# Encoder layer in split fp32 on one core: neighbouring weight pairs multiplied in alternation, and the work beside them spread out

## The chip, the core and the metric

The kernel runs on one core of a Trainium2 chip. TensorE (PE) multiplies, PEld is its loading of the stationary operand; VectorE (DVE), ScalarE (ACT) and GpSimd (POOL) compute, SyncE (SP) issues loads, and POOL also issues the stores. The metric is the device time of one execution in microseconds. The kernel before takes 2571.83 us (median of 3 runs, 2565.88 to 2572.41).

## The reference, cut to what matters

One layer for 512 prompt tokens and 2048 sample tokens, all fp32, 1024 channels:

```
h = rmsnorm(x, norm_pre);  z = h @ w_in                 # 1024 -> 6656
pool_u, pool_g, q, k, v, attn_g, merge = split(z)
pb = (multiscale_pool(pool_u) per group @ w_pool_group) * pool_scale * silu(pool_g)
ab = windowed_attention(rope(q), rope(k), v, sink) * silu(attn_g)
m = sigmoid(merge_p) * (pb @ w_pool_proj) + sigmoid(merge_a) * (ab @ w_attn_proj)
y = x + rmsnorm(m @ w_out, norm_post)
```

The change touches the first half alone: the norm, the projection `z`, and what is done with each column of `z` before it is stored.

## The kernel before, in words

Every fp32 operand is split in two parts, hi and lo (`hi_lo`: ACT rounds it to fp32r, DVE subtracts), and a product is three matmuls (`mm3`, lines 143 to 145).

**Phase 1** is the input projection. The 2560 tokens stand in three blocks (768, 896, 896), the 6656 columns in 26 pairs of 2 x 128 columns. A block times a pair is a 2 x 2 product of halves with seven multiplications in place of eight, M1 to M7, in the order `ORDER = M1, M6, M2, M5, M7, M3, M4`. One such product is 12 matmuls (four slices of K by three) with 384 or 448 moving columns. Its operands are sums of quarters: `X[...]` of the tokens, which lie in `arena` for a block, and `A11, A12, A22, S1` to `S4` of the weights, split product by product into one of seven `w` tiles (`Pair.op`).

Products accumulate in three PSUM banks of a pair: A (`ps_g`, two buffers) holds M1 and then M1+M2, B (`ps_s`, three buffers) M6, then M5, then M3 on top, C M7 and then M4 (`ps_s`, for the second of two joined pairs `ps_o`, of which there is one). After each product something reads the bank, and the next product into the same bank must wait for that reader: M2 waits for `s` (ACT, line 441), M5 for `U2` (DVE, line 444), M3 for `U4` (DVE, line 452), M4 for the sum after M7 (DVE, line 424). In the order above one other product stands between a product and the one that waits for its reader. After M4 `post.finish()` does what the columns need: `Rope` (k and q: six DVE operations on 896 columns, two splits, sixteen stores), `Silu`, `Gate`, `Pool`, `Values`. A pair's results lie in two `z` tiles from its M2 on until they are stored; `finish` takes up to two more, and there are six.

TensorE runs in the order in which the program is written (`manual_schedule`); the other engines' order is set by the framework's scheduler, and each engine runs its queue strictly in that order. `run` issues the weight splits up to seven `w` tiles ahead.

**Beside the products** stands other work, hung into the program with `hook` and `beside` at a pair and product of a block: squares of the next block's tokens for the norm (`stats_load`, `stats_sum`), forming the next block's token sums (`later_load`, `later_form`, pairs 9 to 17), the pooling of the first block's columns (`late_load`, `late_pool`, from block 1, pair 13), and the splitting of the second phase's weights (`split_load`, `split_form`, block 2, pairs 6 to 23). All of them load into the four `h` tiles. A piece is loaded at one product and used three products later.

**The start.** `first_stats` squares the first block's eight token slices on ACT, and TensorE sums each over the partitions (48 matmuls against `ones`). Then `rstd`, `prep_r` (the scale, transposed), `normed`, and the first operands `X`. `fold` multiplies `w_pool_group` into the projection's pooling columns: eight items of four steps, each item three raw tiles (`u` or `h`), three `w` tiles, and 24 matmuls with 256 columns; its results (`wpool`) are the weights of the pooling pairs. 12 of the 32 steps run ahead of pair 0, the other 20 between the products of pairs 0 and 1.

**Phase 2** (attention, three projections, the last norm) is not touched.

Of the kernel before, what the change touches and what calls it, by code (L numbers as in the profile page):

```python
# [28 lines left out]
NPAIR = 26  # L29
# [9 lines left out]
S_AT, T_AT, V_AT, PERIOD = (0, 1, 3, 5), (3, 5, 8), (9, 11, 13), 12  # L39
CUTS = (28, 46, 64)  # L40
PUTS0, PUTS = (8, 14, 20, 26, 40, 44, 60, 62), (2, 5, 8, 11, 16, 20, 44, 48)
NW, NZ, NH, NR = 7, 6, 4, 3


@with_exitstack
def encoder(ctx, tc, a, out):
# [19 lines left out]
    def utile():  # L66
        return sb.tile([128, 512], F32, tag="u", bufs=4, name="u")
# [106 lines left out]
    def fold():  # L174
        steps = []

        def raw_split(src, n):
            raw = utile() if n < 3 else htile()
            nc.sync.dma_start(raw, src)
            w = wtile()  # L180
            hi_lo(w[:, 0, :], w[:, 1, :], raw)
            return w

        for g in range(4):
            for half in range(2):
# [24 lines left out]
    ssqs = {}  # L210

    def first_stats(k, x):

        t0, t1 = BLOCKS[0][0] // 128, BLOCKS[0][1] // 128
        n = t1 - t0
        if k == 0:
            ssqs["p"] = psum("g")
        if k % 2 == 0:
            ssqs["q"] = qtile() if k < 4 else rope_tile().rearrange("p a b -> p (a b)") if k < 6 else row_tile()
        o = k % 2 * 128 * n if k < 6 else 0  # L220
        sq = ssqs["q"][:, o:o + 128 * n]
        A.activation(sq, x[:, 0:128 * n], AF.Square)
        for t in range(n):
            T.matmul(ssqs["p"][:, t:t + 1], lhsT=sq[:, t * 128:(t + 1) * 128], rhs=ones, start=k == 0 and t == 0, stop=k == 7, skip_group_check=True)
        if k == 7:
            ssqs[0] = sb.tile([128, 16], F32, tag="ssq", bufs=2, name="ssq")
            V.tensor_copy(ssqs[0][:, 0:n], ssqs["p"][:, 0:n])

    def stats_load(s, ts):
        if s not in ssqs:  # L230
# [440 lines left out]
    def phase1():  # L671
        prog = []
        fs = fold()
        fold0 = fs[0][0], fs[4][0]
        forming = first_operands()
        xs0 = {}
        n0 = BLOCKS[0][1] // 128
# [1 line left out]
        def first():  # L679
            cst["ident"] = load([128, 128], a["ident"], "ident")  # L680
            cst["gpre"] = load([128, NKT], a["norm_pre"], "gpre")
            next(forming)
            fold0[0].load()
            next(forming)
            rstd(0)
            fold0[1].load()
            pairs[0].raw()
            pairs[1].raw()

        def second():  # L690
            prep_r(0)
# [43 lines left out]
        hooks = {}  # L735
# [1 line left out]
        def hook(s, i, j, f):  # L737
            hooks.setdefault((s, i, j), []).append(f)

        def beside(s, i, load, form, j=0):  # L740
            box = {}
            hook(s, i, j, lambda: box.update(x=load()))
            hook(s, i, j + 3, lambda: form(box["x"]))

        for s in range(len(BLOCKS)):
            hook(s, 1, 6, lambda s=s: load_rope(s, "rope_q"))
# [5 lines left out]
            for i, t in zip((4, 5, 6, 7), range(t0, t1, 2)):  # L752
                ts = range(t, min(t + 2, t1))
                beside(s, i, lambda s=s, ts=ts: stats_load(s + 1, ts), lambda x, s=s: stats_sum(s + 1, x))
            hook(s, 7, 5, lambda s=s: rstd(s + 1))
            hook(s, 8, 2, lambda s=s: prep_r(s + 1))
            for i, (k, c) in zip((9, 10, 11, 12, 14, 15, 16, 17), [(k, c) for k in range(4) for c in range(2)]):
                beside(s, i, lambda s=s, k=k, c=c: later_load(s + 1, k, c), lambda x, s=s, k=k, c=c: later_form(s + 1, k, c, x))
# [6 lines left out]
        for f, (s, i) in enumerate(((1, 13), (1, 18), (1, 19), (1, 20), (1, 21), (1, 22), (2, 4), (2, 5))):  # L765
            for j in range(2):
                beside(s, i, lambda f=f, j=j: late_load(f, j), lambda x, f=f, j=j: late_pool(f, j, x), 3 * j)
        for u in range(48):
            beside(2, 6 + u % 18, lambda u=u: split_load(u), lambda x: split_form(*x), u // 18)
# [11 lines left out]
        fs = fs[12:]  # L781
        duos = [[0, 1]] + [[i] for i in range(2, NPAIR - 2)] + [[NPAIR - 2, NPAIR - 1]]
        for s in range(len(BLOCKS)):
            prog.append((None, lambda s=s: load_rope(s, "rope_k")))
            for duo in duos:
                at = [NPAIR * s + i for i in duo]
                steps = [pair_steps(pairs[i], posts[i], j) for j, i in enumerate(at)]
                last = at[-1] + (1 if len(at) == 2 else 2)
                for j in range(7):
                    for x in steps:  # L790
                        prog.append(x[j])
                    if j == 0:
                        prog.append((None, lambda last=last: fetch_weights(last)))
                    for i in duo:
                        prog += [(None, f) for f in hooks.get((s, i, j), [])]
                    if j > 0:
                        prog += fs[:4]
                        fs = fs[4:]
        return prog

    def split_load(i):
# [414 lines left out]
```

## Time and profile before

| | us |
|---|---|
| median of 3 runs | 2571.83 |
| the profiled execution | 2567.62 |
| its span, first to last instruction | 2565.9 |
| start, up to the first product of pair 0 | 0 to 48.6 |
| pairs 0 and 1 of block 0, with 20 fold steps | 48.6 to 124.7 |
| block 0, pairs 2 to 25 | 124.7 to 524.3 |
| block 1, 26 pairs | 524.3 to 1011.2 |
| block 2, 26 pairs | 1011.2 to 1527.0 |
| phase 2 | 1527.0 to 2565.9 |

The bounds are the starts of the first matmuls in the trace. Profile durations of one matmul overlap the next one's, so that what a matmul costs is read from start to start, or from a count over a stretch without waits.

### The profile page before, as it was taken

What the parts mean: (1) busy time and instruction counts of PE and PEld (TensorE: products, weight loads), DVE (VectorE), ACT (ScalarE), POOL (GpSimd) and SP (SyncE); (2) the same over time, 40 slices, a digit from 0 to 9 for tenths busy, and PEclk for the clock granted to TensorE, in tenths of its full rate; (3) what the DMA queues carried; (4) which work ended last, traced back from release to release, by engine and by line L of the source; (5) the groups of instructions that cost most, each with busy time, mean ns of one, the idle gap of its engine ahead of it and who ended that gap; (6) DMA issues with size and microseconds to landing.
All of it is one profiled execution on the core that took longest, in us unless ns stands there. A gap on an engine that the chain in (4) does not pass through costs nothing. (4 is left out here: it accounts for less than half of the span.)

```text
span 2565.9 us, 34997 instructions
## 1 busy us (share of the span) xinstructions
PE 2375.0 (93%) x11764; PEld 2113.1 (82%) x11764; DVE 1783.8 (70%) x3464; ACT 1158.0 (45%) x2517; POOL 482.5 (19%) x1003
## 2 busy tenths in 40 slices
PE   7789889999998999998889899999999999989998
PEld 6789789998987888887788897788788778878887
DVE  4677676876777787776666657788588488658732
ACT  4444333454333335434443335666366366446511
POOL 1232231112113120313232201110110111011011
PEclk9899999999999999998999999999999999999999
DMA  5586666677567466657786659777787887867684
GB/s 182 180 286 231 238 224 216 227 252 233 189 221 236 163 205 222 217 197 261 266 284 223 224 197 309 245 262 273 256 269 241 284 264 245 285 219 254 238 297 170
DMA packets 204420, 608.43 MB, mean 237 GB/s; under 512 B 28624, under 2 KB 49104, under 8 KB 194256
## 3 DMA queue, kind: packets, MB, share of 16 engines
q1 hardware_dynamic: 158624, 425.44, 50.6%
q0 software_dynamic: 45616, 180.76, 19.1%
q8 instruction: 92, 1.51, 0.2%
q14 instruction: 88, 0.72, 0.1%
HBM read 425.38 MB, written 180.72 MB: 236 GB/s over the span
## 5 line engine op out<-in xcount | busy, mean ns | idle before, releaser
L143 PE MATMUL ps_s<-arena,w 128*128 128x448 f32 (+1 forms) x1512 | 557.4, 369 | 99.4 <-DVE u L452 55.0
L144 PE MATMUL ps_s<-arena,w 128*128 128x448 f32 (+1 forms) x1512 | 549.5, 363 | 0.0
L145 PE MATMUL ps_s<-arena,w 128*128 128x448 f32 (+1 forms) x1512 | 548.6, 363 | 0.9 <-DVE w L106 0.9
L143 PE MATMUL ps_g<-arena,w 128*128 128x512 f32 (+2 forms) x1264 | 493.0, 390 | 18.6 <-ACT s L441 16.2
L145 PE MATMUL ps_g<-arena,w 128*128 128x512 f32 (+2 forms) x1264 | 477.3, 378 | 3.6 <-DVE w L106 3.6
L144 PE MATMUL ps_g<-arena,w 128*128 128x512 f32 (+2 forms) x1264 | 477.7, 378 | 0.0
L143 PEld LDWEIGHTS ps_s<-arena,w 128*128 128x128 f32 x1512 | 294.3, 195 | 131.4 <-DVE u L452 62.0
L105 ACT CAST w<-Q 128x512 fp32r<-128x512 f32 x312 | 192.2, 620 | 336.8 <-PE ps_s L145 303.5
L145 PEld LDWEIGHTS ps_s<-arena,w 128*128 128x128 f32 x1512 | 293.6, 194 | 17.0 <-DVE w L106 1.7
L144 PEld LDWEIGHTS ps_s<-arena,w 128*128 128x128 f32 x1512 | 294.3, 195 | 14.4
L143 PEld LDWEIGHTS ps_g<-arena,w 128*128 128x128 f32 x1264 | 240.4, 190 | 40.8 <-ACT s L441 20.2
L145 PEld LDWEIGHTS ps_g<-arena,w 128*128 128x128 f32 x1264 | 240.0, 190 | 38.7 <-DVE w L106 3.9
L144 PEld LDWEIGHTS ps_g<-arena,w 128*128 128x128 f32 x1264 | 240.8, 191 | 18.8
L1033 ACT ACTIVATE R<-ps_s,nm 128x384 f32<-128x384 f32 (+1 forms) x320 | 179.2, 561 | 149.6 <-DVE nm L1031 142.3
L106 DVE TENSOR_TENSOR w<-Q,w 128x512 fp32r<-128x512 f32 x312 | 213.5, 686 | 38.1 <-ACT w L105 28.7
L106 DVE TENSOR_TENSOR w<-R,w 128x512 fp32r<-128x512 f32 x234 | 160.3, 686 | 69.8 <-ACT w L105 67.9
L1031 DVE CUSTOM_DVE_ANT_0 ps_s<-ps_s,mask,nsink 128x384 f32<-128x384 f32 (+1 forms) x320 | 189.1, 593 | 19.9 <-PE ps_s L1028 17.5
L105 ACT CAST w<-R 128x512 fp32r<-128x512 f32 x234 | 144.6, 620 | 109.4 <-PE ps_s L145 91.6
L106 DVE TENSOR_TENSOR Q<-ps_t,Q 128x512 fp32r<-128x512 f32 x224 | 153.5, 686 | 15.2 <-ACT Q L105 12.8
L1055 PE MATMUL ps_t<-ident,R 128*128 128x128 f32 x896 | 138.6, 276 | 25.2 <-DVE Q L106 21.3
L1055 PEld LDWEIGHTS ps_t<-ident,R 128*128 128x128 f32 x896 | 111.0, 142 | 51.1 <-DVE Q L106 23.3
L105 ACT CAST Q<-ps_t 128x512 fp32r<-128x512 f32 x224 | 130.0, 582 | 36.6 <-PE ps_t L1055 35.1
(229 smaller groups left out, 3762.1 us busy)
## 6 DMA issues: line engine op xcount, KB each, us to landing
Q<-sw SPq DMA_DIRECT2D x52, 1024.0 KB, 5.9
R<-in_w_h SPq DMA_DIRECT2D x54, 768.0 KB, 6.8
w<-w_pp SPq DMA_DIRECT2D x80, 512.0 KB, 4.8
w<-w_ap SPq DMA_DIRECT2D x80, 512.0 KB, 4.3
w<-w_out SPq DMA_DIRECT2D x72, 512.0 KB, 4.5
sw<-Q POOLq DMA_DIRECT2D x26, 1024.0 KB, 7.0
arena<-q SPq DMA_DIRECT2D x20, 1024.0 KB, 7.3
q<-z POOLq DMA_DIRECT2D x128, 112.0 KB, 2.8
```

Source lines behind the costliest of these rows:

```text
L105: A.copy(hi, src)
L106: V.tensor_sub(lo, src, hi.bitcast(F32))
L143: T.matmul(o, lhsT=xs[0], rhs=ys[0], start=start, stop=False, skip_group_check=more)
L144: T.matmul(o, lhsT=xs[0], rhs=ys[1], start=False, stop=False, skip_group_check=more)
L145: T.matmul(o, lhsT=xs[1], rhs=ys[0], start=False, stop=stop, skip_group_check=more)
L1031: V.tensor_tensor_reduce(s, s, mask[:, kb0 * 128:kb1 * 128], -1.0, nsink[:, H:H + 1], ALU.add, ALU.min, nm[:, h:h + 1])
L1033: A.activation(P[:, 0:nk], s, AF.Exp, bias=nm[:, h:h + 1], scale=-1.0, accum_out=l[:, h:h + 1])
L1055: T.transpose(tp[:, h * 128:(h + 1) * 128], pr[h][:, i * 128:(i + 1) * 128], cst["ident"])
```

## The change

- **Order of the products.** Of the pairs 2 to 23 of a block each begins half a pair (seven places) after the one ahead of it, so that the products of two neighbours alternate: M1 of the next, M7 of this one, M6 of the next, M3 of this, M2 of the next, M4 of this, M5 of the next, and so on. Pairs 0 and 1, 24 and 25 alternate as before, place by place. All pairs 2 to 23 use `ps_o` for bank C.
- **The work beside the products** is a row of tasks per block (12, 24 and 28 of them), spaced evenly between the places given in `TASKS` (of 182 places that the pairs take, seven for each); a task's use stands just ahead of the next task's load. Weight splits of phase 2 go two to a task.
- **First statistics.** The squares are added on VectorE into one tile, and TensorE sums that tile alone (6 matmuls).
- **Fold.** 16 of the 32 steps run ahead of pair 0 (2 of them ahead of `prep_r`), none within pairs 0 and 1; the other four items follow the third product of pairs 3, 5, 7 and 9 of block 0. Raw tiles alternate between `u` and `h`. The first four items and both first pairs are loaded ahead of the statistics.

```diff
+TASKS = ((40, 164), (36, 164), (36, 176))
 def fold():
-            raw = utile() if n < 3 else htile()
+            raw = (htile, utile)[n % 2]()
 def first_stats(k, x):
         A.activation(sq, x[:, 0:128 * n], AF.Square)
-        for t in range(n):
-            T.matmul(ssqs["p"][:, t:t + 1], lhsT=sq[:, t * 128:(t + 1) * 128], rhs=ones, ...)
+        if k:
+            V.tensor_add(ssqs["a"], ssqs["a"], sq)
         if k == 7:
+            p = psum("g")
+            for t in range(n):
+                T.matmul(p[:, t:t + 1], lhsT=ssqs["a"][:, t * 128:(t + 1) * 128], rhs=ones, start=True, stop=True)
 def phase1():
+        def task(s, load, form):
+            box = {}
+            tasks[s].append((lambda: box.update(x=load()), lambda: form(box["x"])))
...
-        prog += fs[0:4]
+        prog += fs[0:2]
         prog.append((None, second))
-        prog += fs[4:8]
+        prog += fs[2:16]
         prog.append((None, third))
-        prog += fs[8:12]
...
+            for i in range(NPAIR):
+                edge = i < 2 or i >= NPAIR - 2
+                steps = pair_steps(pairs[NPAIR * s + i], posts[NPAIR * s + i], i % 2 if edge else 1)
                 for j in range(7):
+                    seq.append((2 * j + (i % 2 if i < 2 else 7 * i if not edge else 14 * NPAIR + i % 2), i, j, steps[j]))
+            t0, t1 = TASKS[s]
+            n = len(tasks[s])
+            for k, (begin, form) in enumerate(tasks[s]):
+                t = t0 + (t1 - t0) * k / n
+                seq.append((t, None, 0, begin))
+                seq.append((t + (t1 - t0) / n - 0.01, None, 0, form))
+            for _, i, j, x in sorted(seq, key=lambda v: v[0]):
...
+                if s == 0 and j == 2 and i in (3, 5, 7, 9):
+                    k = 16 + 2 * (i - 3)
+                    prog += fs[k:k + 4]
```

How the instructions move shows in three places. The first is the head of TensorE's queue (before with -, now with +): line 224, now 228, is the sum of the squares over the partitions, `ps_t<-w` the first fold step.

```order
-L1212 UNCONDITIONAL_BRANCH
-L224 MATMUL ps_g<-ones,Q 128x1 x24
-L224 MATMUL ps_g<-ones,rope 128x1 x12
-L224 MATMUL ps_g<-ones,rbc 128x1 x12
-L143 MATMUL ps_t<-w 128x256
+L1233 UNCONDITIONAL_BRANCH
+L228 MATMUL ps_g<-ones,rbc 128x1 x6
```

Of 48 such matmuls six are left.

The second is VectorE's queue in block 1 where the Rope pair 8 ends and pair 9 goes on. Before: line 424 is the reader of pair 8's last product (M4), lines 535 to 540 its rotation, `z<-z` on line 106 its splits, 444 the reader of pair 9's M6, on which its M5 waits.

```order
L424 TENSOR_TENSOR z_6156<-ps_s_6190,u_6138 128x448
L539 TENSOR_TENSOR z_6155<-z_6155,rope_5190 128x896
L536 TENSOR_TENSOR z_6237<-z_6156,rope_5190 128x896
L106 TENSOR_TENSOR w_6264<-R_5979,w_6264 128x512
L537 TENSOR_TENSOR z_6236<-z_6236,z_6237 128x896
L538 TENSOR_TENSOR z_6156<-z_6156,rope_5190 128x896
L106 TENSOR_TENSOR w_6290<-R_6117,w_6290 128x512
L540 TENSOR_TENSOR z_6156<-z_6156,z_6155 128x896
L106 TENSOR_TENSOR z_6236<-z_6236,z_6237 128x896
L444 TENSOR_TENSOR u_6306<-ps_s_6293,s_6280 128x448
```

Now, from the same reader of pair 8's M4 (line numbers are three higher): 455 reads pair 9's M5, and the last row is the reader of pair 9's M7.

```order
L427 TENSOR_TENSOR z_6105<-ps_o_6196,u_6070 128x448
L107 TENSOR_TENSOR w_6322<-R_5881,w_6322 128x512
L539 TENSOR_TENSOR z_6291<-z_6105,rope_5156 128x896
L455 TENSOR_TENSOR u_6337<-ps_s_6213,s_6187 128x448
L540 TENSOR_TENSOR z_6290<-z_6290,z_6291 128x896
L541 TENSOR_TENSOR z_6105<-z_6105,rope_5156 128x896
L107 TENSOR_TENSOR w_6339<-Q_6191,w_6339 128x512
L543 TENSOR_TENSOR z_6105<-z_6105,z_6104 128x896
L107 TENSOR_TENSOR z_6290<-z_6290,z_6291 128x896
L107 TENSOR_TENSOR w_6362<-R_6189,w_6362 128x512
L107 TENSOR_TENSOR z_6105<-z_6105,z_6104 128x896
L427 TENSOR_TENSOR z_6260<-ps_o_6365,u_6337 128x448
```

The rotation is the same work, but pair 9 is at its fifth product where before it was at its second.

The third is SP's queue behind the start. Before, fold items (`in_w_pool_group`, `in_wu_t`) were loaded in a row here, into `h`, ahead of the weights (`R`) of pair 2:

```order
L389 DMA A21_1220<-in_w_h 128x512
L179 DMA h_617<-in_w_pool_group 128x512
L179 DMA h_622<-in_wu_t 128x512
L179 DMA h_627<-in_wu_t 128x512
L179 DMA h_760<-in_w_pool_group 128x512
L179 DMA h_765<-in_wu_t 128x512
L179 DMA h_770<-in_wu_t 128x512
L385 DMA R_665<-in_w_h 128x1536
```

Now the fifth and sixth item stand between the weights of pairs 3 to 8:

```order
L392 DMA A21_1322<-in_w_pg 128x512
L180 DMA h_1097<-in_w_pool_group 128x512
L180 DMA h_1102<-in_wu_t 128x512
L180 DMA h_1107<-in_wu_t 128x512
L388 DMA R_1079<-in_w_h 128x1536
L388 DMA R_1319<-wpool1_100 128x1024
L388 DMA R_1319<-in_w_pg 128x512
L392 DMA A21_1455<-in_w_h 128x512
L180 DMA u_1457<-in_w_pool_group 128x512
L180 DMA u_1462<-in_wu_t 128x512
L392 DMA A21_1656<-in_w_h 128x512
L180 DMA u_1467<-in_wu_t 128x512
```

A load of a fold item that waits for its tile now holds up weights of later pairs behind it.

## Rows read from the trace of the kernel before

**Rows 1.** The page's parts 1 and 2: busy time by engine, TensorE's clock in tenths.

```profile
PE 2375.0 (93%) x11764; PEld 2113.1 (82%) x11764; DVE 1783.8 (70%) x3464; ACT 1158.0 (45%) x2517; POOL 482.5 (19%) x1003
...
PEclk9899999999999999998999999999999999999999
```

**Rows 2.** Stretches: us, busy us (instructions) by engine, granted clock, DMA share, GB/s.

```profile
0.00:48.60 48.60, 36.08 (x174) 33.94 (x175) 16.34 (x28) 21.26 (x37) 8.48 (x14) 0.94 0.59 201
48.60:124.70 76.10, 55.86 (x290) 50.89 (x289) 54.03 (x97) 34.84 (x68) 19.04 (x27) 0.84 0.52 175
124.70:524.30 399.60, 366.02 (x2037) 360.13 (x2036) 298.95 (x537) 168.08 (x318) 99.98 (x181) 0.97 0.69 238
524.30:1011.20 486.90, 457.22 (x2207) 419.69 (x2206) 356.71 (x582) 200.62 (x360) 107.10 (x209) 0.97 0.62 209
1011.20:1527.00 515.80, 463.52 (x2200) 422.73 (x2199) 351.31 (x549) 209.72 (x362) 127.33 (x251) 0.96 0.67 233
```

**Rows 3.** The same view: four pairs of block 0, one of block 1.

```profile
391.50:449.80 58.30, 58.30 (x338) 58.30 (x337) 40.65 (x70) 23.45 (x43) 6.41 (x12) 1.00 0.62 217
655.35:672.15 16.80, 16.80 (x85) 15.77 (x85) 12.01 (x17) 7.29 (x12) 1.09 (x2) 1.00 0.38 138
```

**Rows 4.** Waits of TensorE, 124.7 to 1527: us in total, times, longest.

```profile
PE ps_s L143 <- DVE u L452: 55.0, 20, 6.4
PE ps_s L143 <- DVE u L444: 37.0, 18, 6.1
PE ps_g L143 <- ACT s L441: 16.2, 10, 3.1
PE ps_s L143 <- DVE z L424: 7.1, 7, 2.2
```

**Rows 5.** VectorE in order of time, end of pair 8, block 1: start, us.

```profile
690.58 0.61 DVE L424 TENSOR_TENSOR z<-ps_s,u 128x448 f32<-128x448 f32 x1
...
695.72 0.68 DVE L106 TENSOR_TENSOR w<-R,w 128x512 fp32r<-128x512 f32 x1
696.32 1.08 DVE L540 TENSOR_TENSOR z<-z 128x896 f32<-128x896 f32 x1
697.32 1.08 DVE L106 TENSOR_TENSOR z<-z 128x896 fp32r<-128x896 f32 x1
698.32 0.61 DVE L444 TENSOR_TENSOR u<-ps_s,s 128x448 f32<-128x448 f32 x1
```

**Rows 6.** Waits of TensorE, 680 to 700.

```profile
PE ps_s L143 <- DVE u L444: 1.9, 1, 1.9
```

**Rows 7.** POOL in order of time: the stores of the same pair.

```profile
696.08 2.02 POOL L99 DMA_DIRECT2D q<-z  x4 [6.58 <-ACT z L105]
698.69 5.95 POOL L99 DMA_DIRECT2D q<-z  x12 [0.59 <-DVE z L106]
```

**Rows 8.** DMA issues: queue, count, KB each, median us to landing.

```profile
q<-z POOLq DMA_DIRECT2D x128, 112.0 KB, 2.8
```

**Rows 9.** The start in order of time: squares (ACT), sums (PE), statistics (DVE).

```profile
12.47 0.84 ACT L222 ACTIVATE rbc<-z 128x768 f32<-128x768 f32 x1
24.38 0.84 ACT L222 ACTIVATE rbc<-z 128x768 f32<-128x768 f32 x1 [11.06 <-PE ps_g L224]
6.21 10.40 PE L224 MATMUL ps_g<-ones,Q 128*128 128x1 f32 x48 [6.21 <-ACT Q L222]
25.27 2.72 PE L224 MATMUL ps_g<-ones,rbc 128*128 128x1 f32 x12 [0.99 <-ACT rbc L222]
28.03 0.16 DVE L227 COPY ssq<-ps_g 128x6 f32<-128x6 f32 x1 [27.14 <-PE ps_g L224]
```

**Rows 10.** TensorE in order of time: two fold matmuls.

```profile
37.31 0.28 PE L143 MATMUL ps_t<-w 128*128 128x256 f32 x1
37.43 0.28 PE L144 MATMUL ps_t<-w 128*128 128x256 f32 x1
```

**Rows 11.** Waits of TensorE, 0 to 124.7.

```profile
PE ps_t L143 <- ACT w L105: 16.9, 7, 7.4
```

More of the change, by code (lines that the diff above doesn't have):

```diff
@@ L216, in first_stats @@
         if k == 0:
[L217 to L221, printed above, removed]
+            ssqs["a"] = row_tile()[:, 0:128 * n]
+            ssqs["q"] = [qtile() for _ in range(2)]
+        o = k // 2 % 2 * 1024
+        sq = ssqs["q"][k % 2][:, o:o + 128 * n] if k else ssqs["a"]
         A.activation(sq, x[:, 0:128 * n], AF.Square)
-        for t in range(n):
-            T.matmul(ssqs["p"][:, t:t + 1], lhsT=sq[:, t * 128:(t + 1) * 128], rhs=ones, start=k == 0 and t == 0, stop=k == 7, skip_group_check=True)
+        if k:
+            V.tensor_add(ssqs["a"], ssqs["a"], sq)
         if k == 7:
+            p = psum("g")
+            for t in range(n):
+                T.matmul(p[:, t:t + 1], lhsT=ssqs["a"][:, t * 128:(t + 1) * 128], rhs=ones, start=True, stop=True)
             ssqs[0] = sb.tile([128, 16], F32, tag="ssq", bufs=2, name="ssq")
-            V.tensor_copy(ssqs[0][:, 0:n], ssqs["p"][:, 0:n])
+            V.tensor_copy(ssqs[0][:, 0:n], p[:, 0:n])
     def stats_load(s, ts):
@@ L673, in phase1 @@
         fs = fold()
-        fold0 = fs[0][0], fs[4][0]
+        fold0 = [fs[4 * k][0] for k in range(4)]
         forming = first_operands()
@@ L682, in first @@
             next(forming)
-            fold0[0].load()
+            for k in range(4):
+                fold0[k].load()
+            pairs[0].raw()
+            pairs[1].raw()
             next(forming)
             rstd(0)
-            fold0[1].load()
-            pairs[0].raw()
-            pairs[1].raw()
         def second():
@@ L738, in hook @@
             hooks.setdefault((s, i, j), []).append(f)
-        def beside(s, i, load, form, j=0):
+        tasks = [[], [], []]
+        def task(s, load, form):
             box = {}
-            hook(s, i, j, lambda: box.update(x=load()))
-            hook(s, i, j + 3, lambda: form(box["x"]))
+            tasks[s].append((lambda: box.update(x=load()), lambda: form(box["x"])))
         for s in range(len(BLOCKS)):
@@ L751, in phase1, with stats, form @@
             t0, t1 = BLOCKS[s + 1][0] // 128, BLOCKS[s + 1][1] // 128
-            for i, t in zip((4, 5, 6, 7), range(t0, t1, 2)):
+            for t in range(t0, t1, 2):
                 ts = range(t, min(t + 2, t1))
[L754 to L758, printed above, removed]
+                def stats(x, s=s, last=t + 2 >= t1):
+                    stats_sum(s + 1, x)
+                    if last:
+                        rstd(s + 1)
+                task(s, lambda s=s, ts=ts: stats_load(s + 1, ts), stats)
+            for k in range(4):
+                for c in range(2):
+                    def form(x, s=s, k=k, c=c):
+                        if k + c == 0:
+                            prep_r(s + 1)
+                        later_form(s + 1, k, c, x)
+                    task(s, lambda s=s, k=k, c=c: later_load(s + 1, k, c), form)
             hook(s, NPAIR - 3, 6, lambda s=s: fetch_operand(s + 1, XOP[ORDER[0]]))
@@ L763, in phase1 @@
                     hook(s, NPAIR - 1, j, lambda s=s, r=ORDER[j + 1]: fetch_operand(s + 1, XOP[r]))
-        for f, (s, i) in enumerate(((1, 13), (1, 18), (1, 19), (1, 20), (1, 21), (1, 22), (2, 4), (2, 5))):
+        for f in range(8):
             for j in range(2):
-                beside(s, i, lambda f=f, j=j: late_load(f, j), lambda x, f=f, j=j: late_pool(f, j, x), 3 * j)
-        for u in range(48):
-            beside(2, 6 + u % 18, lambda u=u: split_load(u), lambda x: split_form(*x), u // 18)
+                task(1 if f < 6 else 2, lambda f=f, j=j: late_load(f, j), lambda x, f=f, j=j: late_pool(f, j, x))
+        for u in range(0, 48, 2):
+            task(2, lambda u=u: [split_load(u + i) for i in range(2)], lambda x: [split_form(*y) for y in x])
         hook(0, 3, 0, lambda: nc.sync.dma_start(cst["mask"], a["mask"]))
@@ L775, in phase1 @@
         prog.append((None, first))
-        prog += fs[0:4]
+        prog += fs[0:2]
         prog.append((None, second))
-        prog += fs[4:8]
+        prog += fs[2:16]
         prog.append((None, third))
-        prog += fs[8:12]
-        fs = fs[12:]
-        duos = [[0, 1]] + [[i] for i in range(2, NPAIR - 2)] + [[NPAIR - 2, NPAIR - 1]]
         for s in range(len(BLOCKS)):
             prog.append((None, lambda s=s: load_rope(s, "rope_k")))
[L785 to L788, printed above, removed]
+            seq = []
+            for i in range(NPAIR):
+                edge = i < 2 or i >= NPAIR - 2
+                steps = pair_steps(pairs[NPAIR * s + i], posts[NPAIR * s + i], i % 2 if edge else 1)
@@ new lines, in phase1 @@
+            t0, t1 = TASKS[s]
[5 more added lines that the diff above has]
+            for _, i, j, x in sorted(seq, key=lambda v: v[0]):
+                if i is None:
+                    prog.append((None, x))
+                    continue
+                prog.append(x)
+                if j == 0 and i not in (0, NPAIR - 2):
+                    last = NPAIR * s + i + (1 if i in (1, NPAIR - 1) else 2)
+                    prog.append((None, lambda last=last: fetch_weights(last)))
+                prog += [(None, f) for f in hooks.get((s, i, j), [])]
+                if s == 0 and j == 2 and i in (3, 5, 7, 9):
+                    k = 16 + 2 * (i - 3)
+                    prog += fs[k:k + 4]
```

9 lines of the change are left out of this document (removed).

## The prediction

> **What bounds the kernel now.** I read the page first: TensorE is busy 93% of the span, the next engine 70%, and its clock row has a digit under 9 in few slices [rows 1]. So the kernel is a row of matmuls, and a gain must come from the time between them. Busy time can't show that time, since matmul records overlap; so I cut the span at the first matmuls of the stages and counted [rows 2]. Then I looked for a stretch in which TensorE waits for nothing: four pairs of block 0 (336 matmuls; the few more in the row's count overlap its edges) take 58.3 us, 14.6 a pair or 2.08 a product of 12; one pair with 448 columns takes 16.8 us, 2.4 a product [rows 3]. These are the floors. Against them stand
>
> - block 0, pairs 2 to 25: 399.6 - 24 x 14.6 = 49 us over,
> - block 1: 486.9 - 26 x 16.8 = 50 over,
> - block 2: 515.8 - 437 = 79 over,
>
> together 178 us, and besides 124.7 us for a start whose two pairs need 29. Phase 2 is left alone.
>
> What the 178 us are, the waits tell: 55.0 + 37.0 + 16.2 + 7.1 = 115 us in 55 waits, all for the reader of the PSUM bank that the next product goes into, none for a weight or a transfer [rows 4]. The rest is mostly what follows a wait: the granted clock is 0.97, 0.97 and 0.96 in the three blocks [rows 2], so 12 + 15 + 21 = 48 us at the lower level (1.2 in place of 2.4 GHz), while in the stretches without waits it is 1.00 [rows 3]. Together that is 163 of the 178; the 20 small transposes and the waits too short to be listed are the remainder.
>
> One such wait followed to its cause: after pair 8 of block 1 VectorE reads M4 at 690.58 and then works through the rotation until 698.3; pair 9's U2, on which its M5 waits, is behind it in the queue and read at 698.32 [rows 5], and TensorE stands for 1.9 us [rows 6]. No engine is short of time there; the work comes in a lump, and a product has only one other product, 2.1 to 2.4 us, to cover it.
>
> **The change part by part.** *Alternation.* Between a product and the one that waits for its reader now stand three others in place of one: two products more, 4.2 us in block 0 and 4.8 in the others. The longest waits are 6.4, 6.1, 3.1 and 2.2 us [rows 4]. Only the handful over 4.2 to 4.8 survives, with 1.5 to 2 us each; I put 6 us. One wait is new: bank C of all inner pairs is `ps_o`, of which there is one, so M7 of the next pair waits for the reader of M4 with two products between. That is one product more than now; The two busiest readers have 38 waits with 92 us; were they of one length, 2.1 to 2.4 us less each would leave 8; they are uneven, up to 6.4, and I take 26 for the two, 13 for the one. The clock loss goes with the waits: 48 x 19/115 = 8 us. Against this stands that VectorE gets the same work in less time. It is busy 299 of 400, 357 of 487 and 351 of 516 us [rows 2]; in blocks at their floor that is 299/350, 357/437 and 351/437, 80 to 85% in place of 68 to 75%, and its queue is longer when a reader joins it. Bounds: nothing more waits (0), or half of the 178 stays (89). I take 20, nearer to the low end, since pairs 16 to 19 at 40.65/58.3 = 70% wait not at all [rows 3], and since the lumps that make the waits are of 8 us [rows 5], of which three products cover 6 to 7. So 6 + 13 + 8 + 20 = 47 us of the 178 remain: **-131 us**.
>
> *Even tasks.* They add no instruction. A load and its use lie one task's interval apart: 124/12 places in block 0, 128/24 and 140/28 in the others, with 2.08 and 2.4 us a place 21, 13 and 12 us, where now it is three products, 6 or 7 us. I count nothing for it: what it gives, fewer lumps on ACT and VectorE, is in the 20 us above. What it risks is the four `h` tiles, which a task holds for this long.
>
> *First statistics.* Now TensorE's sums hold back the squares: the seventh is taken at 12.47, the eighth at 24.38 after 11.06 us of waiting, and the statistics are copied at 28.03 [rows 9]. Without it the eighth follows its data, at 13.4 to 14.5. VectorE adds seven times; an addition lies between 0.68 us (512 columns) and 1.08 (896) [rows 5], and all but the last stand beside the squares. Then six matmuls; now 48 take 21 us in the trace's 96 records [rows 9], so 2.7. The copy comes at about 18: 10 us earlier. VectorE is idle at that time and the 7 us cost nothing.
>
> *Fold.* Ahead of pair 0 stand 16 steps in place of 12: 24 matmuls at 0.12 us [rows 10], twice that at the lower clock, 3 to 6 us. Pair 0 then starts at 48.6 - 10 + 4 = 43. Pairs 0 and 1 lose 20 steps (120 matmuls, 14 to 29 us) and most of 16.9 us of waits for fold tiles [rows 11]. They need 29 us of TensorE and 54.0 of VectorE [rows 2], of which 15 subtractions of 0.68 us for fold tiles go: 44. VectorE is the bound, as the operands of the seven products are formed there; I take 47, with 44 and 76 as bounds. So pair 2 starts at 90 in place of 124.7. Given back later: four items, 96 x 0.12 = 12 us of matmuls, and their waits. Each needs three raw tiles that readers (`u`) or tasks (`h`) use too. The nearest row is a fold step's longest wait now, 7.4 us [rows 11]; bounds 0 and one task interval, 21 us, for each. I take 3 for each, 12 in all, because the queue ahead of it is seven tiles deep. Start and fold: -35 + 12 + 12 = **-11 us**.
>
> Sum: the profiled execution took 2567.6 (span 2565.9); less 131 and 11 that is 2425.6. The median of the runs is 4 us above the profiled one, so I forecast **2427 us**.
>
> The Trainium skill has a rule against alternating banks ("TensorE: Matmul & The Clock Gate", section on psum-queue depth-cycling): a kernel that goes round its PSUM banks leaves TensorE idle for moments between groups so often that the clock swings between its levels. The trace doesn't bear it out: the products already change bank from one to the next, and with all readers in time the clock is 1.00 [rows 3]. By the page the sum would be that of the last rival below.
>
> **The rivals.**
> *VectorE becomes the bound*, half of the excess stays: 2571.8 - 89 - 11 = 2472. For it: 80 to 85%, strict order, and readers that stand in the queue ahead of ready work until a product ends. Against it: the stretch at 70% without a wait. 18%.
>
> *The moved fold items wait* a whole task interval each, as a task's `h` tiles are held until its use: 4 x 21 - 12 = 72 us more, 2499. For it: the raw tiles come from the same four. Against: only two of the four items use `h`, and the first stands ahead of the first task. 7%.
>
> *Everything goes*: no wait beyond 20 us, start at VectorE's floor, fold tiles in time: 2571.8 - 158 - 26 = 2388, or a little under. 15%.
>
> *The z tiles set the pace, and it is slower.* A pair holds its two `z` from M2 over eight further products in place of four, and the second pair after it wants them six products after its M4: 14.4 us. A Rope pair's stores are issued until 698.69 + 5.95 = 704.6 [rows 7] and land 2.8 later [rows 8], 17 us after its M4 was read at 690.6 [rows 5]; half of them have landed after 13. Then the copy of M2's columns stands on ACT, or a pooling pair's on VectorE, with readers behind it that have 5 to 7 us to spare. So nothing is lost up to about 20 us, and 78 us for every us beyond, if it holds at all pairs. From 22 us the gain is gone; at 22.5 it is 2427 + 195 = 2622. Against it: 17 us is the longest finish there is, and POOL is busy for a quarter. 4%.
>
> *Swinging clock*: at the mean of 0.84 that pairs 0 and 1 now have [rows 2], the matmuls of the three blocks take (350 + 437 + 437)/0.84 = 1457 us in place of 1224, and the 8 us of clock loss counted above go: 2427 + 225 = 2652. For it: alternation changes the bank at every product. Against it: so does the order now, at 1.00 [rows 3]. 1%.
>
> **How the numbers follow.** Forecast 55%, VectorE 18%, everything 15%, fold 7%, z tiles 4%, clock 1%. The bounds of the forecast's own terms (0 to 89 for the denser queue, 0 to 84 for the fold waits, 44 to 76 for two pairs) give 2395 to 2470 when not all go one way; the next case above reaches 2500, the one below 2375. I give 2378 to 2500 for 8 in 10. A measurement of this kernel tells 0.3%, 8 us, from no change. Only the z tiles and the clock can end there or above, and part of them ends below: faster 0.94, same 0.02, slower 0.04.
>
> **What would show it.** In the profile after: first M1 near 43, pair 2 near 90; the waits on the `U2` and `U4` readers (now lines 447 and 455) under 25 us together, a new one on `ps_o`; granted clock 0.98 or 0.99 in the blocks, which take about 385 (with four folds), 450 and 455 us; VectorE over 78% there. Wrong if TensorE's waits are for `w` tiles, for `z` stores (through ACT line 480 or VectorE 584), or in fold steps of more than 5 us each, or if the blocks keep their length though the readers are in time.

## The result and the profile after

The changed kernel takes 2491.16 us (median of 4 runs, 2490.35 to 2500.71); against the kernel before on the same chip the ratio is 0.9692, 95% interval 0.9656 to 0.9728. The forecast was 2427, in a range of 2378 to 2500: faster, as forecast, but with 64 us of the gain missing. Here and below times and ratios are those of fast runs; of `no_alternation` two more executions (2898 and 5886 us) were in a slower state and are left out. The profiled execution spans 2488.8 us. Parts 1 and 2 of its page answer to [rows 1]:

```profile
PE 2339.5 (94%) x11680; PEld 2088.2 (84%) x11680; DVE 1775.2 (71%) x3471; ACT 1147.7 (46%) x2517; POOL 485.1 (19%) x1003
...
PEclk9899999999999999999899999999999999999999
```

The page alone would hardly show that anything happened. The view by stretches does; it is cut as [rows 2] were, at the first matmuls of the stages (start; pairs 0 and 1; block 0 from pair 2; block 1; block 2; phase 2):

```profile
0.00:38.15 38.15, 18.48 (x115) 17.21 (x116) 23.83 (x36) 22.58 (x37) 9.70 (x16) 1.00 0.80 279
38.15:80.07 41.92, 35.16 (x170) 31.74 (x169) 41.56 (x79) 22.02 (x46) 6.26 (x10) 0.88 0.47 160
80.07:483.16 403.09, 378.15 (x2132) 375.11 (x2132) 305.98 (x554) 176.92 (x338) 112.88 (x197) 0.96 0.73 250
483.16:954.35 471.19, 450.88 (x2207) 418.03 (x2206) 351.96 (x581) 196.26 (x360) 109.29 (x209) 0.98 0.65 215
954.35:1450.30 495.95, 458.20 (x2199) 419.24 (x2198) 345.16 (x550) 206.24 (x362) 126.18 (x251) 0.97 0.70 243
1450.30:2488.80 1038.50, 998.63 (x4866) 826.85 (x4864) 706.73 (x1674) 523.68 (x1375) 120.82 (x323) 0.98 0.77 258
```

Pair 2 starts at 80.1 in place of 124.7, 44.6 us earlier. Block 0 has not become shorter (403 for 399.6, now with four fold items), block 1 gives 16 us and block 2 20. Over the prediction's floors for the blocks there are 53 + 34 + 59 = 146 us, where the forecast had 47, and 24 for the folds. Phase 2 is as long as it was.

The waits of TensorE in the three blocks (80 to 1450; us in total, times, longest), which answer to [rows 4]:

```profile
PE ps_o L144 <- DVE z L427: 50.7, 20, 5.3
PE ps_s L144 <- DVE u L447: 16.7, 9, 3.4
PE ps_t L144 <- ACT w L106: 7.9, 1, 7.9
PE ps_g L144 <- ACT s L444: 6.7, 4, 3.4
```

The largest wait of before, for `U4` (now line 455), is gone. `U2` has 16.7 of 37.0 left, and the wait on the one `ps_o` is new and stands first. The third row is a fold item.

### The profile page after: what moved, and what is told of

It is laid out like the page before. It is cut to its first block, busy times and chain, and to the rows that moved or that the text cites. A ratio compares the mean times of both kernels' runs of the same rounds, so it can differ in the third digit from the quotient of the medians.

```text
span 2488.8 us, 34964 instructions
## 1 busy us (share of the span) xinstructions
PE 2339.5 (94%) x11680; PEld 2088.2 (84%) x11680; DVE 1775.2 (71%) x3471; ACT 1147.7 (46%) x2517; POOL 485.1 (19%) x1003
## 4 chain that ended last, share of the span: by engine, by line
PE 33%; DVE 6%; DMA 5%; issue 4%; ACT 2%; POOL 1%; SPq 0%; POOLq 0%; ACTq 0%; DVEq 0%
PE ps_g L144 5%; PE ps_g L145 5%; PE ps_g L146 5%; PE ps_t L1076 3%; PE ps_s L144 2%; PE ps_s L146 2%; PE ps_s L145 2%; PE ps_o L1091 2%; PE ps_o L1090 2%; PE ps_s L1048 1%; DVE ps_s L1052 1%; PE ps_s L1049 1%; DMA h<-ab 1%; DVE Q L107 1%; PE ps_t L144 1%
## 5 line engine op out<-in xcount | busy, mean ns | idle before, releaser
L144 PE MATMUL ps_s<-arena,w 128*128 128x448 f32 (+1 forms) x984 | 355.4, 361 | 20.8 <-DVE u L447 16.7
L145 PE MATMUL ps_s<-arena,w 128*128 128x448 f32 (+1 forms) x984 | 353.7, 359 | 2.7 <-DVE arena L107 2.7
L146 PE MATMUL ps_s<-arena,w 128*128 128x448 f32 (+1 forms) x984 | 352.7, 358 | 0.0
L144 PE MATMUL ps_o<-arena,w 128*128 128x448 f32 (+1 forms) x576 | 213.6, 371 | 50.7 <-DVE z L427 50.7
L144 PEld LDWEIGHTS ps_s<-arena,w 128*128 128x128 f32 x984 | 188.1, 191 | 35.1 <-DVE u L447 19.8
L145 PE MATMUL ps_o<-arena,w 128*128 128x448 f32 (+1 forms) x576 | 210.8, 366 | 0.0
L146 PE MATMUL ps_o<-arena,w 128*128 128x448 f32 (+1 forms) x576 | 210.5, 365 | 0.0
L1052 DVE CUSTOM_DVE_ANT_0 ps_s<-ps_s,mask,nsink 128x384 f32<-128x384 f32 (+1 forms) x320 | 188.9, 593 | 20.3 <-PE ps_s L1049 18.1
L145 PEld LDWEIGHTS ps_s<-arena,w 128*128 128x128 f32 x984 | 188.1, 191 | 13.2 <-DVE arena L107 4.4
L146 PEld LDWEIGHTS ps_s<-arena,w 128*128 128x128 f32 x984 | 188.1, 191 | 8.9
L144 PEld LDWEIGHTS ps_o<-arena,w 128*128 128x128 f32 x576 | 112.6, 195 | 63.4 <-ACT w L106 26.6
```

The lines of the kernel that those rows point to most:

```text
L144: T.matmul(o, lhsT=xs[0], rhs=ys[0], start=start, stop=False, skip_group_check=more)
L145: T.matmul(o, lhsT=xs[0], rhs=ys[1], start=False, stop=False, skip_group_check=more)
L146: T.matmul(o, lhsT=xs[1], rhs=ys[0], start=False, stop=stop, skip_group_check=more)
L1052: V.tensor_tensor_reduce(s, s, mask[:, kb0 * 128:kb1 * 128], -1.0, nsink[:, H:H + 1], ALU.add, ALU.min, nm[:, h:h + 1])
```

## One late reader, followed

The view in order of time around 1190, in block 2 (start, us; in brackets idle time before and what ended it), ACT, VectorE, TensorE and its weight load:

```profile
1192.77 0.62 ACT L106 CAST h<-h 128x512 fp32r<-128x512 f32 x1 [2.75 <-DMA w_pp<-h]
1195.00 0.62 ACT L106 CAST h<-h 128x512 fp32r<-128x512 f32 x1 [1.61 <-DMA w_pp<-h]
1195.52 0.61 ACT L106 CAST w<-R 128x512 fp32r<-128x512 f32 x1
...
1190.06 0.69 DVE L107 TENSOR_TENSOR w<-R,w 128x512 fp32r<-128x512 f32 x1 [0.99 <-ACT w L106]
1193.42 0.69 DVE L107 TENSOR_TENSOR h<-h 128x512 fp32r<-128x512 f32 x1 [2.67 <-ACT h L106]
1195.65 0.69 DVE L107 TENSOR_TENSOR h<-h 128x512 fp32r<-128x512 f32 x1 [1.53 <-ACT h L106]
1196.26 0.61 DVE L427 TENSOR_TENSOR z<-ps_o,u 128x448 f32<-128x448 f32 x1
...
1186.96 0.36 PE L146 MATMUL ps_o<-arena,w 128*128 128x448 f32 x1
1191.76 0.36 PE L146 MATMUL ps_g<-arena,w 128*128 128x448 f32 x1
1197.02 0.71 PE L144 MATMUL ps_o<-arena,w 128*128 128x448 f32 x1 [4.90 <-DVE z L427]
1196.99 0.29 PEld L144 LDWEIGHTS ps_o<-arena,w 128*128 128x128 f32 x1 [5.24 <-ACT w L106]
```

The product in `ps_o` ends at 1187, and its reader comes at 1196.26. From 1190.7 on VectorE is idle but for two operations: a split of a phase-2 weight (`h<-h`) heads its queue. ACT, which makes the first half of that split, stands for an `h` tile whose last content (`w_pp<-h`) is still being stored. TensorE finishes the two other products it may do, and then stands for 4.90 us. VectorE's own work is not what is late here: each queue runs in its order, and a task's transfer stands at the head.

The weight load of the same product was late too. Its row names ACT's split of the weights (`w<-R`), which stood behind the same task and ended at 1196.13, the reader at 1196.87: by these rows an earlier reader alone would have won some 0.7 of the 4.9 us. The waits of the weight loads at `ps_o` products put 26.6 us in seven of them down to that split.

This case is not all cases. In the 7 us ahead of each of the 20 late readers of `ps_o` VectorE is busy for 20 to 100%. The reader followed is among the four with the least; here it is beside the busiest (VectorE's busy time, then TensorE's clock, DMA share, GB/s):

```profile
1189.26:1196.26 7.00, 2.00 (x4) 0.85 0.94 301
396.86:403.86 7.00, 7.00 (x16) 1.00 0.61 188
```

Ten of the readers, with 32.6 of the 50.7 us, come after less than 60%; the other ten, with 18.1 us, after 72% or more. Whether the work that fills the latter had itself piled up behind a task was not followed.

How did a task come to stand there, though its use was written an interval of some 13 us behind its load? The statistics of block 2, which are taken in block 1, show it: two loads (SyncE's queue) and the squares (ACT) that use them.

```profile
550.36 0.33 SPq L239 DMA_DIRECT2D h<-in_x  x1
558.04 0.33 SPq L239 DMA_DIRECT2D h<-in_x  x1
...
553.44 0.64 ACT L246 ACTIVATE h<-h 128x512 f32<-128x512 f32 x1 [4.11 <-DMA h<-in_x]
...
562.95 0.63 ACT L246 ACTIVATE h<-h 128x512 f32<-128x512 f32 x1 [3.54 <-DMA h<-in_x]
```

The squares stand in ACT's queue for loads issued 3.1 and 4.9 us ahead of them. With all loads and uses of a kind paired in order, the median distance is 5.3 us for squares, 4.8 for token sums and 5.2 for splits. The place in the program orders TensorE alone; on the other engines the scheduler put the uses right behind their loads. The even row exists in the text only.

## The experiments

Unless said otherwise each is the changed kernel with one edit. Runs on different chips are compared by their ratio to the kernel before on the same chip. "Waits" is the sum, in us, of TensorE's wait rows of 1 us and more in the three blocks (from pair 2 of block 0) of the one profiled execution, the fold item's included.

| run | us | ratio [95% interval] | waits |
|---|---|---|---|
| before | 2571.83 | 1 | 115 |
| changed kernel | 2491.16 | 0.9692 [0.9656, 0.9728] | 83 |
| c_alternates | 2477.90 | 0.9630 [0.9591, 0.9669] | 80 |
| no_alternation | 2556.6 | 0.9939 [0.9912, 0.9967] | 118 |
| splits_resident | 2471.46 | 0.9605 [0.9583, 0.9627] | 72 |
| tasks_as_before | 2496.89 | 0.9711 [0.9684, 0.9738] | 86 |
| pinned | 2440.67 | 0.9462 [0.9429, 0.9496] | 48 |
| c_alt_pinned | 2442.68 | 0.9477 [0.9444, 0.9510] | 46 |
| pinned_resident | 2400.69 | 0.9307 [0.9278, 0.9335] | 20 |
| no_alt_pinned | 2502.88 | 0.9711 [0.9679, 0.9743] | 88 |
| pinned_old_tasks | 2461.78 | 0.9554 [0.9519, 0.9589] | 63 |
| pinned_single | 2428.39 | 0.9416 [0.9383, 0.9448] | 40 |
| pinned_h6 | 2407.19 | 0.9354 [0.9311, 0.9397] | 28 |
| h6 | 2441.35 | 0.9494 [0.9466, 0.9521] | 52 |

### Is it the single ps_o?

```diff
-steps = pair_steps(pairs[NPAIR * s + i], posts[NPAIR * s + i], i % 2 if edge else 1)
+steps = pair_steps(pairs[NPAIR * s + i], posts[NPAIR * s + i], i % 2)
```

> Bank C of the inner pairs is ps_s and ps_o in turn, in place of ps_o for all. Theory 1 (the single ps_o, with two products between M4 and the next pair's M7, is where most of the expected gain went: 50.7 us of waits and the lower clock behind them): these waits fall under 10 us, the other readers' waits stay near 25, time 2415 to 2445. Theory 2 (VectorE, with the same work in less time, is late everywhere, and the bank is only where it shows first): the waits come back at the readers of M2, M5 and M3, time 2470 or more.

The wait on `ps_o` goes from 50.7 to 10.2 us, and the sum of the waits stays:

```profile
PE ps_s L144 <- DVE u L447: 23.3, 10, 4.1
PE ps_g L144 <- ACT s L444: 18.4, 9, 2.9
PE ps_s L144 <- DVE u L455: 12.2, 10, 2.3
PE ps_o L144 <- DVE z L427: 10.2, 8, 2.8
```

The intervals of the two ratios overlap, and the waits are back at the readers of M2, M5 and M3, as theory 2 had it; its reason, VectorE's density, is tested below. (The profiled execution, 2488.3 us, is the longest of this kernel's four.) So the single `ps_o` falls as the main cause: the readers are late as a group, and the bank with the least cover shows it first. Weight loads are late here as well: at `ps_s` products they wait 10.2 us in four for ACT's split.

### What the alternation is worth

```diff
-... 7 * i if not edge else 14 * NPAIR + i % 2), i, j, steps[j]))
+... 7 * i if not edge else 14 * NPAIR + i % 2) - (j if 2 <= i < NPAIR - 2 else 0), i, j, steps[j]))
```

> The products of pairs 2 to 23 in the order of before (one pair after the other), all else as changed: start, fold, even tasks, ps_o for bank C. Theory 1 (alternation itself removes the waits on the readers of M2, M5 and M3, 115 us before and 25 now): those waits come back to 80 to 120 us, none on ps_o; only the start's gain stays, time 2530 to 2560. Theory 2 (the 81 us came from the start, 45 us, and from even tasks; alternation gives little): time under 2505.

The two waits of before are back:

```profile
PE ps_s L144 <- DVE u L455: 44.2, 17, 5.7
PE ps_s L144 <- DVE u L447: 41.3, 19, 4.7
```

2556.6 lies inside theory 1's range, though 10.0 us of waits are on `ps_o`. 0.9939 against 0.9692 is 2.5%, 64 us for the alternation, half of the 131 forecast. Start, folds and tasks together are then worth 0.6%, 16 us, where 11 were forecast: pair 2 starts 45 us earlier here too, but block 0 takes 429.8 us for 399.6 before.

### Tasks without their transfers, and at their old places

> The 48 splits of the second phase's weights in block 2 read a resident tile of ones, so that their 48 loads of 256 KB are left out (and the second phase multiplies by ones); ACT, VectorE and the stores do the same work. Theory 1 (a task's first ACT instruction stands at the head of its queue for a transfer that is late, and the weight splits and M4's reader behind it make TensorE wait): block 2 goes from 496 us to 455 to 470, waits on ps_o there under 8 us, blocks 0 and 1 within 2 us. Theory 2 (too much work for VectorE in too little time): block 2 stays above 485.

The edit takes out the load of `split_load`, and the split reads `ones`. Block 2, where the splits are, takes 477 us in place of 496, which lies between the two theories' figures; blocks 0 and 1 take 403 and 474 for 403 and 471. The waits for `ps_o` in block 2, which theory 1 put under 8 us, are hardly fewer than the 22.1 of the changed kernel:

```profile
PE ps_o L144 <- DVE z L427: 18.3, 8, 6.1
```

So these transfers cost something, but most of that wait stays without them; the other transfers of the block were still there.

> The tasks stand at the places that they had before the change, counted in products (pair and product of before), and are used three products after their load; alternation, start and fold as changed. Theory 1 (what stands at the head of ACT's queue is late either way, as the scheduler sets a use where its own clock has the load done): within 15 us of the changed kernel, 2480 to 2510. Theory 2 (even spacing is a good part of the gain): 2515 to 2540, with waits on ps_o and U4 in the old places, pairs 9 to 17 of blocks 0 and 1.

2496.89: no difference from the even row that the intervals could tell. With the timeline above that reads: the even row does not reach the engines.

### Uses held at their place: pinned

A third theory came out of the timeline: readers are late because queues stand for tasks, and they do since the scheduler puts uses right behind their loads. The edit orders what a task computes behind the last reader traced on VectorE (a sum) and on ACT (the copy of `s`, one in each pair); it adds no work (VectorE, ScalarE and GpSimd run 3471, 2517 and 1003 instructions in both kernels).

```diff
+    def behind(f):
+        with contextlib.ExitStack() as es:
+            for x in last.values():            # last reader on VectorE, on ScalarE
+                es.enter_context(tc.issue_after(x))
+            f()
...
-            tasks[s].append((lambda: box.update(x=load()), lambda: form(box["x"])))
+            tasks[s].append((lambda: box.update(x=load()), lambda: behind(lambda: form(box["x"]))))
```

> The changed kernel, with one thing more: what a task computes is queued on VectorE and ScalarE behind the reader of the product at whose place it is written; before, the scheduler put it as early as its data and tiles allowed, right behind its load. Theory 3 (late readers come from queues that stand for the transfers of tasks): a load gets most of an interval, 12 to 21 us, before its use heads a queue; TensorE's waits for readers in the three blocks fall from 82 us to 40 or less, the clock follows, and the kernel takes 2410 to 2450 us. Rival, VectorE's own work is too dense or too lumpy: the work is the same, waits stay at 70 to 85 us, 2480 to 2495. Rival, the single ps_o: its wait stays at about 50 us. Rival that ends above: SyncE's queue now stands for task tiles with weights behind it, waits for w tiles appear, over 2500.

2440.67, inside the theory's numbers. The same squares in block 1, in order of time:

```profile
557.84 6.54 SPq L249 DMA_DIRECT2D h<-in_x  x4
568.13 0.52 SPq L249 DMA_DIRECT2D h<-in_x  x1
...
563.30 0.63 ACT L256 ACTIVATE h<-h 128x512 f32<-128x512 f32 x1 [2.06 <-DMA h<-in_x]
573.89 0.64 ACT L256 ACTIVATE h<-h 128x512 f32<-128x512 f32 x1
...
576.26 0.63 ACT L256 ACTIVATE h<-h 128x512 f32<-128x512 f32 x1
```

The last square of one task still waits 2.06 us for its load; the next task's loads are out by 568.7, and its four squares come from 573.89 on with no idle time before them. VectorE's own waits for tasks in the blocks, first of the changed kernel, then pinned (line numbers ten or two higher):

```profile
DVE h L107 <- ACT h L106: 79.1, 32, 6.4
DVE h L353 <- DMA h<-in_xt: 37.7, 15, 7.8
```

```profile
DVE h L109 <- ACT h L108: 33.7, 19, 7.5
DVE h L363 <- DMA h<-in_xt: 7.3, 5, 3.0
```

And TensorE's waits:

```profile
PE ps_o L146 <- DVE z L437: 17.1, 11, 3.0
...
PE ps_s L146 <- DVE u L457: 8.2, 6, 2.6
PE ps_s L146 <- DVE u L465: 7.3, 5, 2.3
```

With the fold's wait it is 48 us where the theory had 40 or less, and the time is as it had it. None of these rows is a product's wait for a `w` tile, so SyncE did not hold up the weights in a way that shows.

> As the run with pinned tasks, and bank C is ps_s and ps_o in turn as well. Theory 3: with the queues free the single ps_o costs little, so this is within 15 us of the pinned run, at 2405 to 2445. Rival, the single ps_o is what is left: 30 to 50 us under the pinned run.

The same as pinned. With uses pinned the single `ps_o` costs nothing that can be measured.

> As the run with pinned tasks, but all loads of tasks are left out: squares, token sums, pooling of the first block's columns and weight splits read a column of ones that stays in place; each of their operations and stores runs with its size, and what later stages get from them is not the reference's. Theory 3: pinning has already taken most of these waits, so this is 0 to 25 us under the pinned run, with under 25 us of reader waits. If pinning did nothing and the transfers are still the cause: 40 to 70 us under it. If VectorE's density is the cause: the same as the pinned run and as the changed kernel, 2480 to 2495.

40 us under pinned, more than the 25 the theory allowed for: pinning leaves part of the waits. Most of it lies in block 2 (468.1 us pinned), and there a split still comes 5.2 us behind its load in the median, pinned or not, while a square comes 15.6 us behind it in place of 5.3. Without transfers block 2 takes 439.6 us, its floor being 437:

```profile
916.70:1356.27 439.57, 439.48 (x2199) 410.95 (x2198) 342.75 (x543) 208.16 (x358) 127.19 (x251) 1.00 0.69 238
```

VectorE is busy there for 78% of the time with about as many operations (543 for 550), and hardly a reader is late. So work of this density does not by itself make TensorE wait.

### Does pinning do the alternation's work?

> Pinned tasks without alternation: the inner pairs follow one another as before the change. Theory 3 in its strong form (what made readers late before the change, too, were queues that stand for tasks): most of the 108 us of waits of the run without alternation go, and alternation is worth little once tasks are pinned; 2445 to 2475 us, 5 to 35 over the pinned run. Rival, the prediction's reading (lumps of VectorE's own work, which one product cannot cover and three can): pinning gives less here than the 50 us it gave with alternation; 2495 to 2530, 55 or more over the pinned run.

0.0249 over pinned, 64 us, as the rival had it; but pinning gives without alternation what it gives with it (0.9939 to 0.9711, and 0.9692 to 0.9462: 0.023, 59 us), which the rival denied. Neither theory has both, and the strong form of theory 3 falls: of the 118 us of waits without alternation 88 stay when uses are pinned. In total the two add, but that the sums agree so well is partly chance. By the profiled executions pinning takes 32, 1 and 13 us off the three blocks without alternation, and 12, 20 and 28 with it; phase 2, which no edit touches, makes up part of the difference.

### The even row once more, and the tiles

> Pinned tasks, with alternation, but at the places before the change, a use three products (6 to 7 us) after its load. Theory that the even row is worth something only when the scheduler cannot undo it: a load has 6 to 7 us in place of 12 to 21 and its tile, transfer and use collide; waits of 50 to 80 us, 2455 to 2490. Rival, spacing is worth nothing with pinned uses either: 2432 to 2450, like the pinned run.

2461.78, inside the first theory's numbers. With pinned uses the even row is worth 0.9554 - 0.9462 = 0.9%, 24 us (in the old row the weight splits also go one to a task); unpinned it was worth nothing.

> Pinned tasks, weight splits one to a task (48 tasks of one load, one result tile) in place of 24 of two, so that the next load does not need the tiles of the use just ahead of it. If what is left in block 2 (31 us over its floor) is splits that wait for their load: 15 us off it, 2420 to 2432. If it is the copies and stores themselves: the same as the pinned run, 2433 to 2448.

The edit is `for u in range(48)` with one split to a task. 2428.39 is what the first reading gave, but the intervals of 0.9416 and of pinned's 0.9462 overlap, and block 2 is only 6 us shorter (462.4 for 468.1): a small gain, if any.

```diff
-NW, NZ, NH, NR = 7, 6, 4, 3
+NW, NZ, NH, NR = 6, 6, 6, 3
-TILES = 7
+TILES = 6
```

> Pinned tasks, six h tiles in place of four, paid for with one w tile (six in place of seven). If loads that wait for an h tile are what is left: waits for readers fall from 38 us to under 20, 2415 to 2432. If the weight tiles matter more, or SyncE issues the loads no earlier: waits for w tiles appear, 2440 to 2480.

2407.19, under the theory's numbers, and the fastest of these kernels that leaves no load out: 6.5% under the kernel before, 3.5% under the changed one. Its three blocks:

```profile
75.34:461.26 385.92, 373.36 (x2132) 370.75 (x2132) 309.36 (x556) 177.63 (x340) 112.53 (x197) 0.97 0.75 259
461.26:914.00 452.74, 443.55 (x2206) 412.45 (x2206) 355.77 (x587) 203.02 (x365) 110.00 (x210) 1.00 0.68 229
914.00:1362.50 448.50, 442.09 (x2199) 411.94 (x2198) 344.37 (x548) 208.13 (x361) 125.79 (x248) 1.00 0.76 264
```

The readers' waits are 13 us in three rows, and the missing seventh `w` tile shows in the other row, a product that waits for the split of its weights:

```profile
PE ps_s L146 <- DVE u L465: 7.9, 4, 3.4
...
PE ps_s L146 <- ACT w L108: 5.4, 2, 3.5
PE ps_s L146 <- DVE u L457: 3.2, 1, 3.2
...
PE ps_o L146 <- DVE z L437: 2.2, 2, 1.6
```

> The changed kernel with six h tiles and six w tiles, and tasks not pinned. Theory 3: more tiles alone let the scheduler put loads and, right behind them, their uses still earlier; a use still heads its queue while its load is under way, so most of the 82 us of reader waits stay, 2465 to 2495. Rival, what was short were the tiles alone, and pinning only saved tiles: 2405 to 2435, like the run with both. Between (2435 to 2465): each does a part by itself.

The case between: tiles alone give 2.0% of the time before, pinning alone 2.3%, both 3.4%. So theory 3 was wrong to hold that hoisted uses make more tiles worthless. What is left is the wait on `ps_o`:

```profile
PE ps_o L144 <- DVE z L427: 37.2, 12, 5.6
```

The median distance from a load's issue to its use, paired in order as above, and the length of two blocks (us) tell the four kernels apart:

| | squares | token sums | splits | block 1 | block 2 |
|---|---|---|---|---|---|
| changed kernel | 5.3 | 4.8 | 5.2 | 471 | 496 |
| h6 | 6.6 | 8.0 | 5.1 | 448 | 488 |
| pinned | 15.6 | 8.2 | 5.2 | 451 | 468 |
| pinned_h6 | 24.5 | 19.0 | 8.8 | 453 | 449 |

In block 1 either remedy does as much as both; in block 2, where the splits are, it takes both, and only both move a split further from its load.

## Why the prediction was right in direction and 64 us short

The direction followed from the mechanism: alternation took away the waits for `U4` and half of those for `U2`. That 2491 still lies in the range is partly luck, since the part of the range above 2470 was there for the rivals, and none of them is what happened.

- **The bound and the floors** held. 385, 450 and 455 us were forecast for the blocks; pinned_h6, which has two more edits, takes 386, 453 and 449, so the place of the missing time was read rightly.
- **The start** gave more than was forecast. The statistics are copied at 17.5 (forecast 18), after a chain that answers to [rows 9]:

```profile
9.50 5.21 DVE L224 TENSOR_TENSOR rbc<-rbc,Q 128x768 f32<-128x768 f32 x5 [0.54 <-ACT Q L222]
14.76 2.72 PE L228 MATMUL ps_g<-ones,rbc 128*128 128x1 f32 x12 [14.76 <-DVE rbc L224]
17.52 0.17 DVE L230 COPY ssq<-ps_g 128x6 f32<-128x6 f32 x1 [1.61 <-PE ps_g L228]
```

  Pair 0 starts at 38.15 (forecast 43): 20.6 us after that copy, as before, so the four additional fold steps cost nothing that shows. Pairs 0 and 1 take 41.9 (forecast 47), with VectorE busy for 41.56 of it, the bound that was named. Together -44.6 in place of -35.
- **Folds**: 24 us were put down. One wait of 7.9 us, the only one over 1 us, and 12 us of matmuls make 20, without the clock behind that wait. The rival of the fold items names 2499, near the result, but its four waits of 21 us are not there.
- **The alternation** is the step that failed: -131 us against 64 by undoing it. "Only the handful over 4.2 to 4.8 survives" took a wait of before, less the added cover, as the wait after. So `ps_o` was put at 13 us, and it has 50.7, with waits of up to 5.3 although two products cover them. A reader's lateness was treated as a fixed amount. In the case followed it is a queue standing until a transfer ends (9 us from the product's end to the reader at 1196.26), with the weights of the same product behind it; and waits taken from one bank turn up at others (c_alternates).
- **"20 for the denser VectorE"** has the wrong cause. [rows 5] shows lumps of its own work, and from one such row the prediction took all lateness to be that. That holds for some waits at most: ten of the 20 at `ps_o` come after 72% or more of work. In pinned_h6 VectorE is busy for 80, 79 and 77% of the blocks, near the 80 to 85% forecast, and the readers' waits are 13 us. So the rival *VectorE becomes the bound* (2472, 19 us from the result) is not what happened. A term for queues that stand for task transfers was missing: pinning alone takes off 59 us.
- **Even tasks** were counted at nothing and gave nothing, for a reason the prediction did not have. Its sentence that a load and its use lie "21, 13 and 12 us" apart was read from the program; in the trace the medians are 4.8 to 5.3. Pinning and two more tiles, which make that interval real for squares and sums and raise it for splits, give 87 us (0.9692 to 0.9354) where 64 were missing.
- **The clock** term of 8 us is nearer 40 (0.96, 0.98 and 0.97 of the three blocks), because the waits it hangs on stayed: each of the 18 times that the granted clock fell to 1.2 GHz in the three blocks came within a wait or at most 2 us behind one. (The prediction's 48 us "at the lower level" are the time lost; at 0.96 and 0.97 the clock stood at the lower level for about twice as long.) The swinging clock is refuted: pinned_h6 changes the bank at every product and has 1.00 in two blocks. What the Trainium skill says of a kernel that cycles through its banks ("TensorE: Matmul & The Clock Gate", section on psum-queue depth-cycling), that it idles between groups often enough for the clock to swing, is not what this trace shows of changing banks alone.
- **The z tiles**: ACT's copy of M2 (line 480) waits for stores of `z` for 1.9 us in its largest such row. The rival is refuted for the changed kernel. In pinned such waits for the stores of `q` are 18.0 us in seven and in pinned_h6 16.3 in five (longest 6.0); no row of TensorE's waits names that copy.

The 36 us of pinned_h6 in block 0 over its floor can be added up: 12 of fold matmuls, 12.6 of waits (fold steps, transposes, one reader) and some 12 of the clock at 0.97. Still open: whether single splits would add to pinned_h6, and whether another tile than `w` would have been the better price; neither was tried. Its phase 2 takes 1043.7 us for 1038.5 in the changed kernel, but that is no price of the `w` tile that shows: it takes 1037.5 in h6, also with six, and 1042.6 in pinned with seven. How much of the waits without alternation is VectorE's own work and how much queues that stand is open too.

## What to carry to other kernels

Before sizing a late reader by the work ahead of it in its queue, look at whether its engine is busy or idle in that time, and do so for many readers and not for one. If it is idle, look for what stands at the queue's head; where that was a transfer, more cover moved part of the waits to other banks. A place in the program text is no place in an engine's queue where a scheduler may hoist ready work, so read a prefetch distance from the trace, from a load's issue to its use, and pin the use if the distance matters. Two remedies for one wait are worth trying together, and worth reading by stage: pinned uses and two tiles each did as much as both in block 1, and in block 2 it took both.

## What the runs showed of the hardware

The granted clock of TensorE was 1.00 over blocks 1 and 2 of pinned_h6, 450 us each (28 us of waits in its three blocks), and 0.96 to 0.98 in the changed kernel (83 us in three). In block 2 of pinned_h6 VectorE is busy for 77% and the sixteen DMA engines for 76% of the time, and the block ends within 12 us of its floor.
